# A 3x3 convolution on one core: five small reads behind the last store

## The chip, the cores and the metric

The kernel runs on one core of a Trainium2 chip. A core has five engines that run side by side: TensorE (matmuls, "PE" in the profile, with its weight loads as "PEld"), VectorE ("DVE"), ScalarE ("ACT"), GpSimd ("POOL") and SyncE ("SP", which here only issues transfers). Transfers between the chip's memory and the on-chip tiles run on 16 DMA engines, called lanes here. SyncE, ScalarE and GpSimd each have a queue of their own on these lanes: q1 is SyncE's, q10 ScalarE's, q0 GpSimd's.

The metric is the device time of one execution in microseconds (us). A profile is one further execution under the hardware profiler; its span runs from the first to the last instruction.

## The reference

The input has 16 images of 64 channels, 64 by 64; the weights have 128 output channels, 64 input channels and a 3 by 3 window. All are 32-bit floats. The image is padded by one zero on each side.

```
x_pad = np.pad(x, ((0, 0), (0, 0), (1, 1), (1, 1)))
for b, co, ci, kh, kw:
    output[b, co] += weight[co, ci, kh, kw] * x_pad[b, ci, kh:kh+64, kw:kw+64]
```

The output has 16 x 128 x 64 x 64 floats, 33.55 MB; the input is 16.8 MB.

## The kernel before

Images go in pairs: a pair of images with 64 channels each fills the 128 partitions, so there are eight pairs, `p` from 0 to 7. The kernel computes two output rows at a time from four input rows (a Winograd scheme along the height). Three of the products it needs are matmuls over rows of the image itself (tile `xs`, 16-bit), one is over the sums of neighbouring rows (tile `ss`). `Wt` holds the weights, transposed and combined at the start.

*Loads.* SyncE loads the weights (`w_raw`, line 42) and the first two pairs in 32 bits (`x0`, `x1`, lines 44 and 46). GpSimd issues the loads of the other six pairs (line 57), which turn 32-bit numbers into 16-bit ones on the way.

*The main loop* (line 116) runs over the pairs, and in each over four blocks of 16 output rows. In a block TensorE makes three groups of matmuls into PSUM tiles (line 153). ScalarE copies the result of the first group to `ut` (line 167); VectorE adds `ut` to the second and the third group and writes even and odd rows of the output tile `ot` (lines 176 and 179). GpSimd makes the row sums of the next pair (line 71).

*Stores.* Each image of a pair has an output tile of 2 MB. SyncE stores the first image of each pair (line 181). The second image's store is put in a list, `held`, and issued by ScalarE behind the copies of the next block (line 170); what is left in the list goes out at line 185, behind the loop. For the first six pairs a store covers a whole image (2 MB); for the seventh it is cut into halves (1 MB); for the eighth SyncE stores a half and two quarters (1 MB, 0.5 MB, 0.5 MB), and ScalarE two halves. So there are 11 stores on SyncE and 10 on ScalarE. All of them wait for VectorE.

*Order and counters.* A scheduler puts the instructions in order; operations that are wrapped in `keep` stay in the order in which the program names them. Each transfer reports its landing on a counter. The SyncE and ScalarE transfers take eight counters in turn, in program order, and a transfer that takes a counter again first waits until the counter's last transfer has landed. At the end of the program (line 211 in the profile) SyncE waits for all counters, and then all engines meet in a barrier.

*Tiles.* A pool hands out places in the on-chip memory. `const` holds tiles that live to the end; `xpool` has eight image tiles, `opool` seven output tiles of 16 KB a partition, `spool` three tiles of sums and `upool` four of copies.

Of the kernel before, what the change touches and what calls it, by code (L numbers as in the profile page):

```python
# [8 lines left out]
F32 = mybir.dt.float32  # L9
# [4 lines left out]
def kernel(  # L14
# [6 lines left out]
    nc = tc.nc  # L21
# [6 lines left out]
    keep = tc.keep_in_program_order  # L28
    x_rows = x.rearrange("b c h w -> (b c) h w")
# [3 lines left out]
    const = ctx.enter_context(tc.tile_pool(name="const", bufs=1))  # L33
# [76 lines left out]
    def store(eng, p, b2, ot, lo, hi):  # L110
        return eng.dma_start(
            out_rows[2 * p + b2, :, lo:hi, :],
            ot.rearrange("p j i c -> p (j i) c")[:, lo:hi, :],
        )
# [68 lines left out]
                held.append((p, 1, ots[1], *cuts_of[p][1][blk]))  # L183
    while held:
        keep(store(nc.scalar, *held.pop(0)))


# [28 lines left out]
```

## Time and profile before

| | |
|---|---|
| median of 2 runs | 127.26 us (127.19 to 127.33) |
| the profiled execution | 127.28 us |
| its span | 125.5 us |
| mean granted TensorE clock | 0.966 |
| TensorE busy | 106.1 us (85% of the span) |
| VectorE busy | 83.6 us (67%) |
| ScalarE busy | 44.5 us (35%) |
| GpSimd busy | 34.5 us (27%) |
| DMA | 44.48 MB in 4,330 packets, mean 354 GB/s |
| last issue on SyncE | 115.78 us |
| last issue on ScalarE | 116.38 us |

Times inside the execution are counted from the start of the span. A packet is one piece of a transfer on one lane; the 16-KB rows of the big stores are one packet each, the halves have rows of 8 KB and the quarters rows of 4 KB. The number of bytes that GpSimd's loads move is counted at their 16-bit end, so a stretch with many of them shows fewer GB/s at the same share of busy lanes. "Issue to landing" is the time from an instruction that issues a transfer to the last report on its counter.

### The profile page before, as it was taken

The page shows a single profiled execution, that of the slowest core. Times are in us where ns is not written, and L with a number is a line of the kernel's source. Part 1 is how long each engine was busy: PE and PEld are TensorE (multiplying, and loading weights), DVE is VectorE, ACT ScalarE, POOL GpSimd, SP SyncE. Part 2 cuts the span into 40 slices and gives each one's busy share as a digit, 9 for nine tenths or more (in the row PEclk, how much of TensorE's full clock was granted, in tenths as well). Part 3 has the DMA queues.
Part 4 walks back from the last instruction along what each step waited for, and adds up shares of the span by engine and source line. Part 5 has one row for each costly group of instructions (what it writes and reads, how often), then busy time and mean ns, then how long its engine had stood idle before and what let it go on. Part 6 is the DMA issues. An engine that isn't in the chain of part 4 may idle for free.

```text
span 125.5 us, 2411 instructions
## 1 busy us (share of the span) xinstructions
PE 106.1 (85%) x978; PEld 53.1 (42%) x978; DVE 83.6 (67%) x134; ACT 44.5 (35%) x76; POOL 34.5 (27%) x27
## 2 busy tenths in 40 slices
PE   0407999999999999999999999999999999996000
PEld 0303444554545454544455455445545454542000
DVE  0009297787778777777787787888788878768000
ACT  4108937953333333333333333333333333332000
POOL 2840008999357005800490039000000000000000
PEclk9999999999999999999999999999999999999655
DMA  5999999999999999999999999999999999999980
GB/s 150 393 360 329 339 274 211 214 214 185 366 337 386 363 345 360 358 366 347 326 376 376 439 423 418 418 433 428 439 439 418 418 418 420 426 420 431 415 367 30
DMA packets 4330, 44.48 MB, mean 354 GB/s; under 512 B 480, under 2 KB 480, under 8 KB 864
## 3 DMA queue, kind: packets, MB, share of 16 engines
q1 hardware_dynamic: 2016, 21.27, 40.7%
q10 hardware_dynamic: 1440, 16.78, 31.5%
q0 software_dynamic: 864, 6.29, 24.6%
q8 instruction: 7, 0.11, 0.3%
q14 instruction: 3, 0.02, 0.0%
HBM read 17.07 MB, written 33.55 MB: 403 GB/s over the span
## 4 chain that ended last, share of the span: by engine, by line
PE 83%; DMA 7%; DVE 2%; issue 1%; DVEq 0%; SPq 0%
PE acc L153 83%; DMA x<-in_x_dram 7%; DVE ot L176 1%; DVE ss L71 1%; DVE ot L179 0%; DVEq L211 0%; SPq L42 0%; DVEq L176 0%
## 5 line engine op out<-in xcount | busy, mean ns | idle before, releaser
L153 PE MATMUL acc<-xs,Wt 64*128 64x504 f16 (+3 forms) x768 | 88.8, 378 | 0.0
L153 PEld LDWEIGHTS <-Wt 64*128 64x128 f16 x960 | 51.9, 95 | 57.1 <-issue 6.9
L176 DVE TENSOR_TENSOR ot<-acc,ut 128x512 f32<-128x512 f32 x64 | 41.2, 686 | 23.3 <-PE acc L153 18.6
L167 ACT COPY ut<-acc 128x512 f32<-128x512 f32 x64 | 34.4, 589 | 60.9 <-issue 38.5
L179 DVE TENSOR_TENSOR ot<-acc,ut 128x512 f32<-128x512 f32 x64 | 41.1, 684 | 0.0
L71 POOL TENSOR_TENSOR ss<-xs 128x1024 f16<-128x1024 f16 x12 | 25.2, 2122 | 29.2 <-PE acc L153 25.8
L153 PE MATMUL acc<-ss,Wt 64*128 64x504 f16 (+1 forms) x192 | 26.9, 384 | 4.5 <-DVE ss L71 4.5
L71 DVE TENSOR_TENSOR ss<-x 128x512 f16<-128x512 f32 x4 | 2.6, 684 | 9.5 <-DMA x<-in_x_dram 9.5
L71 POOL TENSOR_TENSOR ss<-x 128x1024 f16<-128x1024 f32 x2 | 4.7, 2364 | 11.7 <-DMA x<-in_x_dram 11.7
L96 ACT CAST xs<-x 128x1024 f16<-128x1024 f32 (+2 forms) x4 | 4.0, 1054 | 3.9 <-DMA x<-in_x_dram 3.9
L89 PE MATMUL wp<-ident,w 128*64 128x128 f16 x18 | 1.3, 328 | 4.4 <-POOL w L51 4.4
L173 ACT CAST xs<-x 128x1024 f16<-128x1024 f32 x4 | 4.0, 1058 | 0.0
L57 POOL DMA_DIRECT2D xs<-in_x_dram x6 | 3.4, 582 | 0.0
L89 PEld LDWEIGHTS <-w 128*64 128x64 f16 x18 | 1.1, 210 | 4.4 <-POOL w L51 4.4
L91 ACT CAST Wt<-wp 128x384 f16<-128x384 f32 x1 | 0.5, 478 | 3.0 <-PE wp L89 3.0
L91 ACT ACT_TABLE_LOAD x1 | 1.3, 1283 | 0.7 <-PEq L200 0.7
L51 POOL CAST w<-w_raw 128x576 f16<-128x576 f32 x1 | 0.7, 662 | 2.4 <-DMA w_raw<-in_weight_dram 2.4
L98 ACT CAST Wt<-wp 128x384 f16<-128x384 f32 x1 | 0.5, 478 | 0.5 <-DVE Wt L94 0.5
L93 DVE TENSOR_TENSOR Wt<-wp,Wt 128x384 f16<-128x384 f32 x1 | 0.6, 550 | 0.0
L94 DVE TENSOR_TENSOR Wt<-wp,Wt 128x384 f16<-128x384 f32 x1 | 0.5, 548 | 0.0
L99 ACT CAST Wt<-wp 128x384 f16<-128x384 f32 x1 | 0.5, 485 | 0.0
masks.py:199 POOL TENSOR_SCALAR_AFFINE_SELECT ident<-ident 128x128 f16<-128x128 f16 x1 | 0.3, 292 | 0.1
(5 smaller groups left out, 0.6 us busy)
## 6 DMA issues: line engine op xcount, KB each, us to landing
out_dram<-ot SPq DMA_DIRECT2D x6, 2048.0 KB, 20.2
out_dram<-ot ACTq DMA_DIRECT2D x6, 2048.0 KB, 19.8
xs<-in_x_dram POOLq DMA_DIRECT2D x6, 1024.0 KB, 30.2
x<-in_x_dram SPq DMA_DIRECT2D x2, 2048.0 KB, 13.0
out_dram<-ot ACTq DMA_DIRECT2D x4, 1024.0 KB, 10.6
out_dram<-ot SPq DMA_DIRECT2D x3, 1024.0 KB, 11.3
out_dram<-ot SPq DMA_DIRECT2D x2, 512.0 KB, 9.0
w_raw<-in_weight_dram SPq DMA_DIRECT2D x1, 288.0 KB, 2.9
```

Of the source, the lines that this page charges most:

```text
L51: keep(nc.gpsimd.tensor_copy(w16, w_raw))
L57: keep(nc.gpsimd.dma_start(xs[p], x_rows[128 * p : 128 * p + 128, :, :]))
L71: eng.tensor_add(ss[p][:, lo : lo + n, :], v[:, lo : lo + n, 0, :], v[:, lo : lo + n, 1, :])
L89: nc.tensor.matmul(wp[q : q + 64, k * CO : k * CO + CO], w16[:, t::9], ident)
L91: keep(nc.scalar.copy(wrow(G1), wps[1]))
L93: keep(nc.vector.tensor_sub(wrow(G21), wps[2], wrow(G1)))
L96: keep(nc.scalar.copy(xs[0][:, lo:hi, :], x0[:, lo:hi, :]))
L153: nc.tensor.matmul(tiles[b2][:, lo - j0 : hi - j0, c_lo:c_hi], Wt[p0 : p0 + 64, wi, kw, :], rhs, start=i == 0, stop=i == n - 1,)
L167: keep(nc.scalar.copy(ut, U[b2]))
L173: keep(nc.scalar.copy(xs[1][:, lo : lo + 16, :], x1[:, lo : lo + 16, :]))
L176: nc.vector.tensor_add(ots[b2][:, j0 : j0 + RB, 0, :], A[b2], us[b2])
L179: nc.vector.tensor_add(ots[b2][:, j0 : j0 + RB, 1, :], Bt[b2], us[b2])
```

## The change

Behind the last store a new tile `spare` of 16 partitions is taken from the `const` pool, with five times 16 floats, 320 bytes a partition. SyncE then issues five reads from `x` into it: 64 bytes from each of 15, 12, 9, 6 and 3 rows, into the first partitions. The rows lie 64 channel planes apart in `x`, so each is the start of another image. Nothing reads the tile.

```
     while held:
         keep(store(nc.scalar, *held.pop(0)))
+    spare = const.tile([16, 5, 16], F32)
+    for n, k in enumerate((15, 12, 9, 6, 3)):
+        keep(nc.sync.dma_start(spare[0:k, n, :], x_rows[0 : 64 * k : 64, 0, 0:16]))
```

## The prediction

> **What bounds the kernel now.** I read the table of stretches first, because the edit touches only the end of the program and the question there is what still runs. This is that view of the kernel before; each line gives the stretch, its length, the busy time of the five engines, the granted clock, the share of the 16 DMA lanes that is busy, and GB/s.
>
> ```profile
> 20.00:45.00 25.00, 25.00 (x238) 12.50 (x234) 19.43 (x32) 12.02 (x20) 16.58 (x8) 1.00 1.01 289
> 45.00:70.00 25.00, 25.00 (x237) 12.52 (x235) 19.43 (x32) 8.59 (x16) 8.41 (x4) 1.00 1.02 359
> 70.00:100.00 30.00, 30.00 (x284) 15.03 (x282) 23.74 (x39) 9.92 (x19) 4.21 (x2) 1.00 1.01 429
> 100.00:119.00 19.00, 14.99 (x142) 7.29 (x138) 12.82 (x21) 5.11 (x10) 0.00 (x0) 0.95 1.01 421
> 119.00:122.00 3.00, 0.00 (x0) 0.00 (x0) 0.00 (x0) 0.00 (x0) 0.00 (x0) 0.50 0.93 388
> 122.00:123.30 1.30, 0.00 (x0) 0.00 (x0) 0.00 (x0) 0.00 (x0) 0.00 (x0) 0.50 0.29 123
> 123.30:124.10 0.80, 0.00 (x0) 0.00 (x0) 0.00 (x0) 0.00 (x0) 0.00 (x0) 0.50 0.05 20
> 124.10:125.50 1.40, 0.00 (x0) 0.00 (x0) 0.00 (x0) 0.00 (x0) 0.00 (x0) 0.50 0.00 0
> ```
>
> TensorE shows 25.00 of 25.00 us, but its busy time is modelled; the DMA lanes are full as well (1.01, 1.02), and they are still full when the last matmul has gone. From 115 us on only stores run. From 122 us on most lanes are done; from 123.3 to 124.1 the share is 0.05, about one lane of 16 (0.0625). So **one lagging lane, emptying its part of the stores, sets the end**. The queues' shares say the same of the whole:
>
> ```profile
> q1 hardware_dynamic: 2016, 21.27, 40.7%
> q10 hardware_dynamic: 1440, 16.78, 31.5%
> q0 software_dynamic: 864, 6.29, 24.6%
> q8 instruction: 7, 0.11, 0.3%
> ```
>
> 40.7 + 31.5 + 24.6 + 0.3 = 97.1% of 16 lanes over 125.5 us. The 2.9% left are 3.6 us a lane, of which 1.8 lie before the first packet (the trace has it at 1.77 us) and 1.4 behind the last. Then SyncE's waits and issues:
>
> ```profile
> SPq L211 <- DMA out_dram<-ot: 8.1, 4, 3.0
> ```
>
> SyncE's own closing waits (line 211, the end of the program) take 8.1 us in four pieces: it is idle while the last four stores land. The timeline of SyncE and ScalarE with the time to landing of each issue gives these, issue to landing: SyncE 102.97 to 114.3; ScalarE 103.57 to 115.0; SyncE 109.33 to 119.3; ScalarE 109.93 to 119.7; SyncE about 112.9 to 122.1; SyncE 115.78 to 124.6 (8.8 us); ScalarE 116.38 to 124.0 (7.6 us). SyncE's last half-megabyte store ends last, at 124.5 to 124.6; the closing barriers make up the rest to 125.5.
>
> **The change, part by part.** It removes nothing. It adds five issues on SyncE, and a tile of 320 bytes a partition. In the instruction order of the two built programs, all other engines have the same instructions, and the five reads stand last on SyncE, so no store is queued behind them.
>
> *Issue and waits.* The SyncE and ScalarE transfers take eight completion counters in turn, and a counter is used again only when its last transfer has landed. There are 3 loads and 21 stores, so read n waits for the store eight places before it: reads 1 to 3 for those landed at about 109.8, 114.3 and 115.0, read 4 for the one at 119.3, read 5 for the one at 119.7. An issue costs 0.33 to 0.43 us (lines 111 and 44). The last store's issue ends at 115.78 + 0.33 = 116.1; reads 1 to 3 go out by 116.1 + 3 x 0.33 = 117.1; read 4 goes from 119.3 to 119.7, read 5 from 119.7 to about 120.1. All of this lies in the 8.1 us that SyncE waits anyway, so it costs nothing; without that cover it would be 5 x 0.33 = 1.7 us. Behind the reads on SyncE stand the closing waits, which now also want the reads landed, and the other engines wait for SyncE there.
>
> *Work on the lanes.* 15 + 12 + 9 + 6 + 3 = 45 rows of 64 bytes, 2.9 KB beside 44.48 MB. The nearest rows are the weight load: 128 packets of 2,304 bytes, median 93 ns when data flow, 696 ns the first; a counter's 4-byte write takes 9 ns. So five rows on one lane cost less than 5 x (93 + 9) = 0.5 us. From the same load, issue to landing on empty lanes is 2.9 us. Read 5, issued at 119.7, lands at 119.7 + 2.9 = 122.6; two turns of ScalarE's 8-KB packets before it (309 ns each in the trace) make it 123.2. That is 1.3 us before the last store. **On every lane but the lagging one the reads are hidden.**
>
> *On the lagging lane* the reads stand behind SyncE's last store, which leaves it at 124.08. Nothing in the views names the lane. The price lies between 0 (it carries no row) and 5 x 696 = 3.5 us (it carries five, each waiting out its first-packet time alone). Which end is near? The kernel already mixes reads and writes on full lanes: GpSimd's loads beside stores (20 to 70 us) take a median of 625 ns for 16 KB read, against 611 for a 16-KB store. Reads queued on a busy lane do not show their latency. Reads 1 to 3 have then been queued for 7 us. I take five at the small end, 0.1 us, as the sum.
> The Trainium skill, DMA: Bandwidth & Descriptors, bears on the lane: its section on why a DMA increments its semaphore by 16 puts k rows on the lowest-numbered k engines, and its section "Latency and other measured facts" calls engines 7 and 15 usually the slower ones. No trace here names an engine. If 15 lags, no read is on it and the sum is +0; if 7 lags, three are.
>
> *The new tile.* In the built programs every tile of the loads and stores stood on a multiple of 256 bytes; the 320 bytes shift all of them to 64 bytes behind one. The trace of before shows no store from such a place. The weight tile is the nearest: it stands 128 bytes behind one, and its 93 ns per 2,304 bytes are in line with the other packets. These (159, 309, 611 ns for 4, 8, 16 KB) cost 150 ns per 4 KB and some 9 ns fixed; 2,304 bytes by that are 84 + 9 = 93. So a write to a shifted place costs nothing; a read from one is open. Low end: 0 (a gain below nothing is excluded within half a per cent, since the lanes move at their steady rate at every size). High end: a 16-KB row done as slowly as four packets of 4 KB, 4 x 159 = 636 against 611, 4.1% of the 122.3 us in which lanes run, 5.0 us. I take 0, by the weight tile.
>
> **Sum.** The profiled execution took 127.28 us (span 125.5, 1.78 around it); the runs' median is 127.26. 127.28 + 0.1 = **127.4 us**.
>
> **The rivals.**
> *B, the first read shows its latency.* The lagging lane carries rows and, drained, waits once: 696 - 93 = 0.6, plus the rows' 0.1: 128.0. For it: 15 of 16 lanes carry at least one row. Against it: the 625 ns above.
> *C, the shift slows stores.* If each packet pays its fixed 9 ns once more: 2,688 store packets, 256 of x0 and x1 and 768 of GpSimd's, 232 a lane, 2.1 us, 129.4. The bounds are 127.4 and 132.3. For it: the lanes are full, so every ns counts. Against: the weight tile.
> The Trainium skill, the same page, section "How a descriptor splits into AXI transactions", says that a descriptor that starts off a 256-byte boundary fetches unused bytes from the boundary on: 64 here, two beats of 128 in 4 KB. By 150 / 128 = 1.17 ns a beat that is an estimate of 2.3 ns a packet, 0.5 us in all, 127.9. The aligned cost of the weight tile speaks against it, but that tile is written, not read.
> *D, slower: the reads run one after another* on the lagging lane, each with its full 696 ns because the counter's write parts them. Place: behind 124.08. Price: 3.5 us with five rows, 130.8; it decides from the fourth row on (4 x 0.7 = 2.8 us, over 2%). For it: the first packets of the weight load took up to 696 ns on idle lanes. Against: in the tail, 4-byte counter writes are followed at once by the next packet.
> *E, faster.* With 97.1% of the lanes' time filled and 3.2 of the 3.6 idle us before the first and behind the last packet, there is hardly anything to win.
> That the reads are left unwaited or go out early is excluded by the instruction order and the closing waits.
>
> **How the numbers follow.** Forecast (0 to 0.5 us at the end) 0.57; B 0.16; C 0.13; D 0.11; E 0.03. About 2% (2.5 us) is what a measurement of this kernel can tell from no change. Forecast and B lie within it, and of C about half (0.07): 0.80. Slower: D and the upper half of C, 0.17. Faster: 0.03. The range goes from 127.0 (the runs' scatter below 127.26, and a little of E) to 129.6, which takes in B, the 9 ns of C and two or three rows of D; it leaves out D's four and five rows (0.11), C's upper half (0.06) and E (0.03).
>
> **What would show it.** Reads 1 to 3 issued from 116.1 to 117.1, reads 4 and 5 at 119.3 and 119.7 behind a wait for a store; all landed before 124.5; one lane at the end; 4-, 8- and 16-KB store packets at 159, 309 and 611 ns. If the last packets are reads, B or D holds: one late gap or several. If a stretch like 70 to 100 us falls below 429 GB/s, it is C. The forecast is wrong if a read's landing, not the last store's, releases SyncE.

## The result, and the profile after

The changed kernel takes 128.18 us (two runs, 128.02 and 128.34) against 127.26 before: ratio 1.008, 95% interval 1.006 to 1.010. It is slower by 0.9 us, clear of the scatter and well inside 2%. The profiled execution took 128.34 us with a span of 126.6.

The end of the stretches of the changed kernel (stretch, length, five engines' busy time, clock, share of busy lanes, GB/s):

```profile
119.00:122.00 3.00, 0.00 (x0) 0.00 (x0) 0.00 (x0) 0.00 (x0) 0.00 (x0) 1.00 1.04 424
122.00:123.30 1.30, 0.00 (x0) 0.00 (x0) 0.00 (x0) 0.00 (x0) 0.00 (x0) 0.62 0.83 338
123.30:124.10 0.80, 0.00 (x0) 0.00 (x0) 0.00 (x0) 0.00 (x0) 0.00 (x0) 0.50 0.18 72
124.10:125.20 1.10, 0.00 (x0) 0.00 (x0) 0.00 (x0) 0.00 (x0) 0.00 (x0) 0.50 0.04 15
125.20:126.60 1.40, 0.00 (x0) 0.00 (x0) 0.00 (x0) 0.00 (x0) 0.00 (x0) 0.50 0.00 0
```

The lanes run on to 124.6 in place of 124.1. SyncE's waits at the program's end, and its last issues in the timeline:

```profile
SPq L214 <- DMA spare<-in_x_dram: 2.3, 3, 1.7
```

```profile
117.85 0.33 SPq L111 DMA_DIRECT2D out_dram<-ot  x1
118.23 4.63 SPq L188 DMA_DIRECT2D spare<-in_x_dram  x5
```

Before, SyncE's closing waits named the output, that is, stores. Now all that is left names `spare`: **the landings of the reads release SyncE last**. And the five issues take up 4.63 us from first to last, not the 1.7 us that five issues of 0.33 would.

This execution has a peculiarity that is not the change's. The line of the waits for the first input reads, before and after:

```profile
DVE ss L71 <- DMA x<-in_x_dram: 9.5, 1, 9.5
```

```profile
DVE ss L71 <- DMA x<-in_x_dram: 11.7, 1, 11.7
```

The first input landed 2.2 us later, and everything behind it on the engines moved with it (SyncE's last store went out at 117.85, not 115.78). Another run of the same five reads (`e2_reads_aligned`, below) has 9.5 again and is as slow, so the 2.2 us are not what costs. I read the end of the program from that run, where the tail starts from nearly the same place as before (SyncE's last store goes out at 116.04). In the changed kernel's own profile the case is not clean: the last store in is ScalarE's, at 125.05 against 124.54 for the last one before, and the last three reads follow at 125.08, 125.28 and 125.41. So of the 0.87 us by which the last landing moved there, 0.50 lie ahead of those three reads.

### The profile page after: what moved, and what is told of

Same layout as the page of the kernel before. It is cut to its first block, busy times and chain, and to the rows that moved or that the text cites. A ratio compares the mean times of both kernels' runs of the same rounds, so it can differ in the third digit from the quotient of the medians.

```text
span 126.6 us, 2416 instructions
## 1 busy us (share of the span) xinstructions
PE 105.9 (84%) x978; PEld 54.2 (43%) x978; DVE 83.5 (66%) x134; ACT 44.5 (35%) x76; POOL 34.5 (27%) x27
## 4 chain that ended last, share of the span: by engine, by line
PE 82%; DMA 8%; DVE 2%; issue 1%; DVEq 0%; SPq 0%
PE acc L153 82%; DMA x<-in_x_dram 8%; DVE ot L176 1%; DVE ss L71 1%; DVE ot L179 0%; DVEq L214 0%; SPq L42 0%; DVEq L176 0%
## 5 line engine op out<-in xcount | busy, mean ns | idle before, releaser
L153 PEld LDWEIGHTS <-Wt 64*128 64x128 f16 x960 | 53.1, 95 | 57.4 <-issue 8.2
```

Of the source, the lines that this page charges most:

```text
L153: nc.tensor.matmul(tiles[b2][:, lo - j0 : hi - j0, c_lo:c_hi], Wt[p0 : p0 + 64, wi, kw, :], rhs, start=i == 0, stop=i == n - 1,)
```

## The experiments

"Before" in the table is the median of the kernel before, run alongside. The ratio with its interval is the recorded comparison of the runs; it is not the quotient of the two medians (for `e5_five_16` that would be 1.010). Costs in us below are differences of medians. All reads but those of the changed kernel go into a tile that leaves the other tiles on multiples of 256 bytes (1,280 bytes a partition in the runs `e2` to `e5`, 2,048 in `f` and `g`). The edits are shown against the changed kernel, and most of them leave out the line that takes the tile.

| run | reads behind the last store | us | before | ratio (95% interval) |
|---|---|---|---|---|
| `e1_tile_only` | none, 320-byte tile | 127.31 | 127.28 | 1.0019 (0.9999 to 1.0038) |
| `e2_reads_aligned` | 15, 12, 9, 6, 3 rows | 128.30 | 127.28 | 1.0088 (1.0068 to 1.0108) |
| `e4_one_read_3` | 3 rows | 127.21 | 127.28 | 0.9993 (0.9972 to 1.0015) |
| `e5_five_16` | 5 x 16 rows | 128.54 | 127.28 | 1.0132 (1.0090 to 1.0174) |
| `f1_five_3` | 5 x 3 rows | 127.23 | 127.31 | 0.9996 (0.9973 to 1.0019) |
| `f2_five_6` | 5 x 6 rows | 128.25 | 127.31 | 1.0077 (1.0056 to 1.0098) |
| `f3_one_16` | 16 rows | 127.79 | 127.31 | 1.0032 (1.0012 to 1.0052) |
| `f4_merged` | one transfer, 16 rows of five pieces | 127.79 | 127.31 | 1.0041 (1.0024 to 1.0059) |
| `g1_ladder` | 6, 5, 4, 3 rows | 127.84 | 127.22 | one run |
| `g2_seven_3` | 7 x 3 rows | 128.54 | 127.22 | 1.0083 (1.0051 to 1.0115) |
| `g3_early` | none; 5 x 16 rows earlier | 127.77 | 127.22 | 1.0045 (1.0031 to 1.0059) |
| `g4_on_chip` | 5 x 16 rows, copied on the chip | 128.32 | 127.22 | 1.0086 (1.0071 to 1.0101) |

### The tile or the reads

The edit does two things: it shifts the tiles of images, sums and results by 320 bytes, and it reads. The two are taken apart.

```
-    for n, k in enumerate((15, 12, 9, 6, 3)):
-        keep(nc.sync.dma_start(spare[0:k, n, :], ...))
+    keep(nc.gpsimd.memset(spare, 0.0))
```

> The tile of 320 bytes without the reads; GpSimd fills it once behind its last sum, and GpSimd is idle there. Every other tile stands 64 bytes behind a multiple of 256, as in the changed kernel. If the reads made the 0.9 us (theory R): 127.3 us, ratio 1.000 within 0.2%, and 8-KB and 4-KB packets at means of 311 and 159 ns as before. If the shift of the tiles made it (theory S): 128.0 to 128.3, ratio 1.006 to 1.010, and these packets at means of 315 and 162 ns as in the changed kernel.

```
-    spare = const.tile([16, 5, 16], F32)
+    spare = const.tile([16, 5, 64], F32)
...
-        keep(nc.sync.dma_start(spare[0:k, n, :], ...))
+        keep(nc.sync.dma_start(spare[0:k, n, 0:16], ...))
```

> The same five reads, but into a tile of 1,280 bytes a partition, so that every other tile stands on a multiple of 256 bytes again. Theory R: 128.0 to 128.3, ratio 1.006 to 1.010, and a read's landing releases SyncE at the end. Theory S: 127.3, ratio 1.000. If each has a part, this and the run with the tile alone add up to 0.9 us over before.

The tile alone costs nothing that can be told (1.0019; the interval goes from 0.9999 to 1.0038, so up to 0.5 us is not excluded by the times), and its 8-KB and 4-KB packets have means of 310 to 312 and 159 ns, as before. The reads alone cost all of it (1.0088). So the longer packets of the changed kernel's profile (315 and 162 ns) do not come from the shift, nor from the reads: `e2_reads_aligned` has 310 to 311 and 159. SyncE's closing waits with the reads alone:

```profile
SPq L214 <- DMA spare<-in_x_dram: 4.2, 1, 4.2
```

One wait of 4.2 us, for the first read; when that has landed, the other four follow so closely that no wait of note is left.

### How many rows, and where

```
-    for n, k in enumerate((15, 12, 9, 6, 3)):
+    for n, k in enumerate((3,)):                      # e4_one_read_3
+    for n, k in enumerate((16, 16, 16, 16, 16)):      # e5_five_16
```

> One read, of 3 rows, into the 1,280-byte tile (four reads fewer). If the end is set by a read that stands behind the last store on the lagging lane, three lanes of 16 will mostly miss it: 127.3, ratio 1.000. If any read at the end costs its own round trip, 127.7 or more. By the slow issues seen in the changed kernel (0.40 to 1.20 us each, 4.63 in all), one issue ends at about 117.4 and cannot end last.

> Five reads of 16 rows each, into the 1,280-byte tile: every lane gets one row of each, and SyncE has no missing lanes to report for. Theory R with the lagging lane at fault: 128.1 to 128.6, at or above the five unequal reads, since the lagging lane now surely holds five. If the long issues of the changed kernel (up to 1.20 us) came from row counts below 16, the issues here take 0.33 to 0.45 us each, and the last read is issued at about 120, by the landing it waits for.

A read of 3 rows is free, five of 16 rows cost 1.3 us (their times scatter, from 128.29 to 130.11). The issues did not get faster with 16 rows (0.42 to 1.21 us each), so row counts below 16 are not why they are slow. What the price is made of is told by the landings. This is from the trace's record of the reports on the counters, the last one of each transfer, in us; the first number is the last store's:

```
e2_reads_aligned   124.438 | 124.624  124.812  124.997  125.182
e5_five_16         124.584 | 124.770  124.958  125.144  125.329  125.520
```

**The reports of the reads stand 0.186 us apart, one behind the other, behind that of the last store.** The packets themselves do not: on the lagging lane of `e2_reads_aligned` the store's report leaves at 123.933, and then four pairs of a 64-byte packet (11 ns) and a 4-byte report (9 ns) follow within 0.05 us, the last at 123.985. Only their arrival is drawn out. Four reports follow the store with reads of 15, 12, 9, 6 and 3 rows: the lane gets a row of each but the last.

```
-    for n, k in enumerate((15, 12, 9, 6, 3)):
+    for n, k in enumerate((3, 3, 3, 3, 3)):           # f1_five_3
+    for n, k in enumerate((6, 6, 6, 6, 6)):           # f2_five_6
+    for n, k in enumerate((6, 5, 4, 3)):              # g1_ladder
```

> Five reads of 3 rows each. Theory L: the lagging lane gets a row from the reads of 15, 12, 9 and 6 rows but not from the one of 3, and each row that stands behind the last store there lands 0.186 us after the one before it. By L this run costs nothing: 127.3, ratio 1.000. Rival I: what costs is SyncE's five issues and their waits, or five round trips, on whichever lane: 128.2, ratio 1.007, as with the unequal reads.

> Five reads of 6 rows each. Theory L: the lagging lane is among the three that the sixth, fifth and fourth row reach, so it gets five rows: 5 x 0.186 = 0.93, and two closing checks more than one behind the last landing, (3 - 1) x 0.06 = 0.12: 128.3, ratio 1.008. If the lane lies beyond the sixth row: 127.3.

> Reads of 6, 5, 4 and 3 rows, one look at the landings, to tell which lane lags. Theory L says that it is one of those that the fourth, fifth or sixth row goes to. Its reports, behind the last store's, are 0.186 us apart: three of them if it takes the fourth row (6, 5, 4), two if the fifth, one if the sixth. One time only: 128.0, 127.9 or 127.8, too close to tell them by the time.

Five reads of 3 rows are free, five of 6 cost 0.94 us, as the count of rows on one lane has it; the same five issues on SyncE are in both. The closing waits, first of 3 rows, then of 6:

```profile
SPq L214 <- DMA spare<-in_x_dram: 2.5, 3, 1.6
SPq L214 <- DMA out_dram<-ot: 1.2, 1, 1.2
```

```profile
SPq L214 <- DMA spare<-in_x_dram: 4.1, 1, 4.1
```

With 3 rows the last thing SyncE waits for is a store again; with 6 it is a read. In the profile of `f2_five_6` the last store in is ScalarE's (124.461), and the five reads land behind it from 124.645 to 125.394, again 0.187 apart, as behind SyncE's store in the other runs. In the ladder the last store is in at 124.394, the reads of 6 and 5 rows at 124.580 and 124.767, those of 4 and 3 rows long before (123.196 and 122.541). So the lagging lane is the one that the **fifth** row goes to, in this execution; the counts of the other runs fit a lane from the fourth to the sixth row. The Trainium skill, DMA: Bandwidth & Descriptors, section "Latency and other measured facts", calls engines 7 and 15 usually the slower ones. No trace here names an engine, but neither of the cases that the prediction drew from it fits: it had no read or three of the five on the lagging lane, and there were four.

### The read or its report

```
-    for n, k in enumerate((15, 12, 9, 6, 3)):
+    for n, k in enumerate((16,)):                     # f3_one_16
```

> One read of 16 rows, one on each lane. Theory L: 0.186 for the one row on the lagging lane; and since its counter is the first of eight that SyncE checks at the end, seven checks of 0.06 us follow in place of one: 0.36. Together 0.55: 127.8, ratio 1.004. If only the landings count and the checks cost nothing: 127.5, ratio 1.0015.

```
+    keep(nc.sync.dma_start(spare[0:16, 0:5, 0:16], x_rows[0:1024:64, 0:5, 0:16]))
```

> One read of 16 rows with five pieces of 64 bytes in each: every lane gets the five reads of the run with five times 16 rows, but one report to a counter in place of five. If the 0.186 us belong to the report: as with one read of 16 rows, 127.8, ratio 1.004. If they belong to each 64-byte read: 5 x 0.186 + 0.36 = 1.29: 128.6, ratio 1.010.

```
-        keep(nc.sync.dma_start(spare[0:k, n, 0:16], x_rows[...]))
+        keep(nc.sync.dma_start(spare[0:k, n, 0:16], w_raw[0:k, 0:16]))   # k = 16, five times
```

> Five copies of 16 rows of 64 bytes from the weight tile to the spare tile, in place of the reads of the chip's memory. If the 0.186 us a row belong to the report of a transfer that has to land first: as with five reads of 16 rows, 128.3 to 128.5, ratio 1.008 to 1.013. If they belong to the round trip to the chip's memory: 127.5 to 127.8, with reports close together.

Five pieces on every lane with one report cost what one piece does, 0.48 us both; with five reports they cost 1.26. So the price belongs to the transfer's report, not to the 64 bytes. Copies within the chip cost about the same as reads of its memory (1.0086, interval 1.0071 to 1.0101, against 1.0090 to 1.0174), and the three that land behind the last store (125.032) keep the distance (125.216, 125.401, 125.592): the memory's latency is not it. `f4_merged` has its verdict from the times alone. Its profiled execution is one of those whose first input came late (12.2 us), and there the read had landed before the last store:

```profile
SPq L213 <- DMA spare<-in_x_dram: 4.3, 1, 4.3
SPq L213 <- DMA out_dram<-ot: 1.4, 1, 1.4
```

The Trainium skill, DMA: Bandwidth & Descriptors, section "Queues, rings and completion order", has it that a report lands only after every earlier write of its engine has. That fits reports that come in one by one, but no run here shows what fills the 0.186 us.

The single read of 16 rows shows the second term. From the last landing to the end of the span it took 0.96 us before and 1.33 here. SyncE checks the eight counters in a fixed order, and what stands behind the last landing depends on whose it is:

| last landing on counter | from it to the end, us | seen in |
|---|---|---|
| first | 1.33 | `f3_one_16` |
| second | 1.27 | `g1_ladder` |
| fourth | 1.14 | changed kernel, `e2_reads_aligned` |
| fifth | 1.07 | `e5_five_16`, `f2_five_6`, `g4_on_chip` (1.08) |
| seventh | 0.96, 0.95 | before, `e1_tile_only`, `f1_five_3` |
| eighth | 0.89 | `e4_one_read_3`, `f4_merged` |

That is (1.33 - 0.89) / 7 = 0.063 us a counter. The view of line 214 shows the checks themselves, 28 ns each with a gap behind it. Of the ten on SyncE eight are the checks and two belong to the barrier. In `f3_one_16` (first) all ten crowd into the last 1.3 us; in the kernel before (second) they began at 116.2:

```profile
L214 SPq EVENT_SEMAPHORE  x10: 17/28/28, 124.2 to 125.5; - x10
```

```profile
L211 SPq EVENT_SEMAPHORE  x10: 17/28/28, 116.2 to 125.4; - x10
```

The profiled execution of `f3_one_16` took only 127.33, against a median of 127.79: its last store landed at 124.005, 0.54 us earlier than before, which hides nearly all of the 0.19 for the report and the 0.37 for the checks.

### Later and earlier

```
-    for n, k in enumerate((15, 12, 9, 6, 3)):
+    for n, k in enumerate((3, 3, 3, 3, 3, 3, 3)):     # g2_seven_3
```

> Seven reads of 3 rows, none on the lagging lane. Five such cost nothing. The seventh takes the counter of SyncE's last store and so waits until that has landed, at about 124.5; its issue takes some 0.3 us, and alone on its lane it lands 1.9 to 2.9 us later (the one-read run and the weight load): 126.7 to 127.5, and 0.9 for the end: span 127.7 to 128.5, time 129.4 to 130.2, ratio 1.017 to 1.023. If the counter's wait were not the point: 127.3.

```
     for p in range(NP):
...
+        if p == NP - 1:
+            spare = const.tile([16, 8, 64], F32)
+            for n, k in enumerate((16, 16, 16, 16, 16)):
+                keep(nc.sync.dma_start(spare[0:k, n, 0:16], x_rows[0 : 64 * k : 64, 0, 0:16]))
         ots = [
...
-    for n, k in enumerate((15, 12, 9, 6, 3)):
-        keep(nc.sync.dma_start(spare[0:k, n, :], ...))
```

> The five reads of 16 rows, issued before the last pair's work rather than behind the last store. They wait for stores landed by then; the last three SyncE stores take other counters and so wait for other landings, at most 0.5 us later than their data. Theory L: a report that stands ahead of the last stores is hidden by their data: 127.3 to 127.6, ratio 1.000 to 1.002. If a report held its lane up for 0.186 us wherever it stands: 5 x 0.186 = 0.93, 128.2.

Seven reads of 3 rows cost 1.3 us by the medians, five cost nothing: the counter's wait is real, but cheaper than expected. SyncE's waits at the reads:

```profile
SPq L188 <- DMA out_dram<-ot: 4.3, 4, 2.8
SPq L214 <- DMA spare<-in_x_dram: 0.5, 1, 0.5
```

The seventh read goes out at 123.54, behind the landing of SyncE's last store (123.53 in this execution), and lands at 124.72. A 64-byte read on an idle lane thus takes 1.18 us from issue to landing, 0.24 of it the issue. I had taken 1.9 to 2.9 from transfers that had queued or moved more. The profiled execution is not a typical one: it took 127.45, one of the three fastest of twelve, and eight of the others took 128.4 to 128.9. In it SyncE's last store was in 1.01 us earlier than before (124.54). With the store in at 124.54 the same steps would end 1.01 us later, at 128.5. That is an estimate that meets the median of 128.54; no execution of the common kind was profiled.

The early reads miss both expectations: 0.55 us, where hiding gave 0 to 0.3 and a price wherever they stand gave 0.93. The reads shift the turn of the counters, and stores now wait for older transfers to land, not the 0.5 us that I had reckoned. On SyncE one waits 4.6 us:

```profile
SPq L111 <- DMA out_dram<-ot: 4.9, 2, 4.6
```

The one that matters is on ScalarE. Its store of 109.93 now goes out at 114.13, just behind the landing (114.05) of the last transfer on the counter that it takes. Before, and in `g3_early`:

```profile
109.93 0.34 ACTq L111 DMA_DIRECT2D out_dram<-ot  x1
```

```profile
114.13 0.34 ACTq L111 DMA_DIRECT2D out_dram<-ot  x1
```

While ScalarE is held there it copies nothing, and VectorE waits for its copies. From 100 us on, before and in `g3_early`:

```profile
DVE ot L176 <- ACT ut L167: 0.6, 1, 0.6
```

```profile
DVE ot L180 <- ACT ut L171: 3.0, 2, 2.4
```

So SyncE's last store leaves at 117.09, 1.3 us later than before, yet the last landing is at 124.61 against 124.54, since the lanes had work queued; with the checks that is 0.18 us of span. The profiled execution took 127.49, the fastest of six. Where the rest of the median's 0.55 us lies stays open.

## Why the prediction was right or wrong

**The place was right, the size was not.** The forecast was 127.4, and 128.18 was measured: slower, within 2%, and 0.8 us beyond the forecast, whose own 0.1 us is no more than the scatter of the runs. The reads do stand behind the last store on one lagging lane (SyncE's in `e2_reads_aligned`, ScalarE's in the changed kernel's own profile), the other lanes' reads are free (`f1_five_3`), and SyncE's issues are free. By the sign that the prediction set itself, its mechanism failed: a read's landing, not the last store's, releases SyncE. That 128.18 lies inside the range is owed to the room left for B and for a part of D, not to the sum.

**The step that failed** is the price on the lagging lane: "I take five at the small end, 0.1 us". For the packets it was even too much: a 64-byte packet takes 11 ns, as a busy lane shows no latency. But the sum had no term for what comes after the packet. In the profile of `e2_reads_aligned` (the fastest of its six runs) the last landing is at 125.18 against 124.54 before: four reports of 0.186 are 0.74, and the store before them was 0.10 earlier. The rest of the span is 1.14 against 0.96, 0.18 more, for three more checks of 0.063. 0.64 + 0.18 = 0.82 us, which is the difference of the spans (126.32 and 125.50); the medians differ by 1.0. The trace of before could not give the 0.186: no small transfer stands behind another on a drained lane there. But it held two hints that the sum passed over. The last store's report leaves its lane at 124.08 and lands at 124.54, so a report takes 0.46 us to arrive. And the last two checks start at 124.56 and 124.62, 0.06 apart.

**The issues** were sized by stores (0.33 us) and took 0.40 to 1.20 us in the changed kernel. That moved the plan (reads 4 and 5 never waited for a store in the changed kernel's profile, as the first three issues had eaten the time), but the cover held.

**The rivals.** B named 128.0 and is the nearest in time, by another mechanism: the first read's latency of 0.6 us. `f3_one_16` tells them apart: there the last store's report on the lagging lane is in at 124.005 and the read's at 124.190, 0.19 later and not 0.6; and in `e2_reads_aligned` there is a step for each read and not one for all. C is out from its 2.1 us up (`e1_tile_only`). Its sign, a stretch from 70 to 100 us below 429 GB/s, does show in the changed kernel (424), but the shifted tile alone has 429 again, and `f4_merged`, whose tiles are not shifted and whose first input came late too, has 419. The estimate of 0.5 us that the prediction drew from the Trainium skill, DMA: Bandwidth & Descriptors, section "How a descriptor splits into AXI transactions", is a ratio of 1.004. That is at the edge of the interval of `e1_tile_only`; but it wanted 2.3 ns more a packet, and the 4-KB packets have a mean of 159.2 ns there and 159.0 before. D had the right picture, one read behind another on the lagging lane, but each step is 186 ns and not 696, so that four rows cost 0.74 us and not 2.8. Nothing of E was seen.

## What to carry to other kernels

Where lanes are full to the end, as here, what counts at the end is the lane that empties last, and what stands behind its last piece. In this kernel a small transfer there was priced by its report, 0.19 us each, not by its bytes. So merge small transfers into one (five pieces: 0.48 us with one report, 1.26 with five), or give them so few rows that the lagging lane is not touched, once a trace has shown which lane that is. A transfer that takes a counter still in use waits for a landing: behind the last store that added a read's whole way of 1.18 us, and in the middle of the program it held an engine that had other work (`g3_early`).

## What was not expected of the hardware

- Reports of small transfers on the lagging lane land about 0.186 us apart (0.184 to 0.191 in six profiles), for reads of the chip's memory and for copies on the chip alike, though the packets leave 13 ns apart.
- Issues of 64-byte transfers took 0.24 to 1.52 us on SyncE, where stores of 128 rows took 0.33. The longest mostly stand among the early ones, while stores were queued (1.52 in `g3_early`, 1.17 for the only read of `f3_one_16`); the seventh read of `g2_seven_3`, with SyncE's stores landed, took 0.24. A first read of 3 rows took 0.37 to 0.42, of 15 or 16 rows 0.84 to 1.52, but the merged one of 16 rows 0.52. Why was not tried.
- The first input landed at 9.3 to 9.7 us in eleven profiles and at 10.6 to 12.2 in three, with the same instructions at the start. Up to that point no experiment differs from the kernel before but in the places of tiles. Why was not tried.
